# Attention weights and layer 0's head outputs turned in 32 by 32 blocks on VectorE and through DRAM, in a two-layer transformer trunk

## Chip, core and metric

The program runs on one core of a Trainium2 chip. A core has five engines that run their own instruction queues side by side: TensorE (PE, matmul), VectorE (DVE), ScalarE (ACT), GpSimd (POOL) and SyncE (SP, which here only starts DMAs). The metric is device time in microseconds (us). Lower is better.

## What is computed

Two transformer layers over 256 tokens of width 2048, all in float32. Layer 0 has differential attention (8 heads, each the difference of two softmax maps, then an RMS norm per head), layer 1 has forgetting attention (16 heads); each layer has a squared-ReLU MLP of width 8192. The parts that the change touches:

```python
a = p[:, :, 0] - lam * p[:, :, 1]                  # layer 0: weights of one head
o = jnp.einsum('bhqk,bhkv->bhqv', a, v)            # layer 0: sum over keys k
o = rmsnorm(o, subln_g, SUBLN_EPS) * (1.0 - lambda_init)
h = h + o.reshape(B, S, D_MODEL) @ w_o_a           # sum over the features of o
...
p = jax.nn.softmax(s, axis=-1)                     # layer 1
o = jnp.einsum('bhqk,bhkd->bhqd', p, v)            # layer 1: sum over keys k
h = h + o.reshape(B, S, D_MODEL) @ w_o_b
h = h + jnp.square(jax.nn.relu(rmsnorm(h) @ w_in)) @ w_out
```

TensorE sums over the partition of both operands. The softmax leaves the weights with queries on partitions, and the sum over keys needs keys there. So each head's weights have to be turned, and in layer 0 the outputs too (tokens on partitions, features wanted).

## The kernel before

All matrix products with the large weights run in split precision: a weight block `raw` is cast to `whi` (ACT, `split`, L173), `wlo = raw - whi` is formed (DVE, `split_low`, L176), and TensorE sums three products.

The program is one list of **slots**. A slot is one granule of weights: 512 KB, 128 by 1024. A unit of kind B (`mm_b`) has slots of 12 matmuls of 512 columns; a unit of kind A (`mm_a`) has four slots, with 8, 24, 8 and 24 matmuls. In the attention stages the units follow in the order V (8 slots), q, k, q, k (4 slots each) for two layer 0 heads, or V, k, q, k, q for two layer 1 pairs of heads; so heads follow each other by turns after 8 and 16 slots. Attention itself is cut into small steps that `plan(e)` hangs on later slots (e is the last slot of the head's last unit). Each slot s emits, in this order:

1. `pre[s]`: evacuations,
2. the cast of granule s+4 on ACT,
3. `mid[s]`: DVE steps of attention,
4. `split_low` of granule s+4 on DVE, and then on SP the load of granule s+8 into the `raw` buffer that this has just freed (`NRAW` = 4 buffers, L163),
5. the slot's matmuls,
6. `post[s]`: small PE steps.

Every engine works through its own instructions strictly in that order, so a step that waits holds everything behind it on its engine. The queue of SP holds the weight loads of the whole program.

For a layer 0 head: `scores` in `post[e+2]`, `softmax` in `mid[e+3]` and `mid[e+4]`, `weights` in `mid[e+4]` and `mid[e+5]`, `turn_a` (three TensorE transposes into PSUM) in `post[e+6]`, `keep_a` (an ACT copy to SBUF) in `pre[e+7]`, `av` (the product with V) in `post[e+7]`, `take_o` in `pre[e+8]`, `norm_o` in `mid[e+9]`, `turn_o` (four TensorE transposes) in `post[e+10]`, `split_o` in `pre[e+11]`. Layer 1 works on pairs of heads in the same manner, with six transposes in a `turn_a`; its `av` writes features on partitions, so its outputs need no turn. For the last two of the eight pairs `av` comes later (`e_av`), since V is made last there. At `pre[e+6]` of each second pair but the last, `spread_c` loads the next group's decay table (`NC`, 256 KB and 512 KB) on SP's queue.

Of the kernel before, what the change touches and what calls it, by code (L numbers as in the profile page):

```python
# [20 lines left out]
P = 128  # L21
D = 2048
S = 256
HD = 128
FF = 8192
NA = 8
# [16 lines left out]
def kernel(ctx: ExitStack, tc: tile.TileContext, *args):  # L43
    (x, rel_table, w_qkv, lq1, lk1, lq2, lk2, w_o_a,
     w_k, w_v, w_f, b_f, w_q, w_o_b, w_in, w_out, fin_g, onehot, xt, gcols, out) = args
    nc = tc.nc
# [18 lines left out]
    ident = sb.tile([P, P], F32, tag="ident", name="ident")  # L65
# [56 lines left out]
    g_sub = G[:, 80:82]  # L122
# [3 lines left out]
    pre, mid, post = (defaultdict(list) for _ in range(3))  # L126
# [102 lines left out]
    def split_turned(c, tps, gain, dst, bs=(0, 1)):  # L229
# [5 lines left out]
        for b, j, k in at:  # L235
            nc.vector.scalar_tensor_tensor(out=dst[2 * c + b][:, j, S:2 * S], in0=tps[b][:, j * S:(j + 1) * S],
                                           scalar=gain[:, k:k + 1], in1=dst[2 * c + b][:, j, 0:S],
                                           op0=ALU.mult, op1=ALU.subtract)

    def banks():  # L240
        return [ps.tile([P, 512], F32, tag="tp", name="tp") for _ in range(2)]

# [27 lines left out]
    class Norm:  # L270
# [96 lines left out]
    vt = {}  # L367
# [15 lines left out]
    def qk_done(key, R, tag, then=None):  # L383
# [5 lines left out]
                then(e)  # L389
        return done  # L390

    def diff_head(hd):
        p, hl = hd // 2, hd % 2
        st = {}
# [41 lines left out]
            return run  # L436

        def turn_a():
            t = ps.tile([P, 512], F32, tag="tp", name="tpa")
            nc.tensor.transpose(t[:, 0:P], st["a", 0][:, 0, 0:P], ident)  # L440
            nc.tensor.transpose(t[:, P:2 * P], st["a", 1][:, 0, 0:P], ident)
            nc.tensor.transpose(t[:, 2 * P:3 * P], st["a", 1][:, 0, P:2 * P], ident)
            st["tpa"] = t

        def keep_a():
            t = sb.tile([P, 3 * P], F32, tag="aT", bufs=4, name="aT")
            nc.scalar.copy(out=t, in_=st["tpa"][:, 0:3 * P])
            st["aT"] = t

        def av():  # L450
            o = ps.tile([P, 2, S], F32, tag="sc", name="o")
            a, v = st["aT"], vt["a", p]
            cs = slice(hl * S, (hl + 1) * S)
            nc.tensor.matmul(o[:, 0, :], a[:, 0:P], v[:, 0, cs], start=True, stop=True)
            nc.tensor.matmul(o[:, 1, :], a[:, P:2 * P], v[:, 0, cs], start=True, stop=False)
            nc.tensor.matmul(o[:, 1, :], a[:, 2 * P:3 * P], v[:, 1, cs], start=False, stop=True)
            st["o"] = o

        def take_o():
# [14 lines left out]
                                        scalar2=None, op0=ALU.mult)  # L474

        def turn_o():
            t = ps.tile([P, 512], F32, tag="tp", name="tpo")
            for v in range(2):
                for qt in range(2):
                    nc.tensor.transpose(t[:, (v * 2 + qt) * P:(v * 2 + qt + 1) * P],  # L480
                                        st["osb"][:, qt, v * P:(v + 1) * P], ident)
            st["tpo"] = t

        def split_o():
            d = new_x(f"hx{hd}")
            for v in range(2):
                src = st["tpo"][:, v * S:(v + 1) * S]
                nc.scalar.activation(out=d[:, v, 0:S], in_=src, func=AF.Copy, scale=g_sub[:, v:v + 1])
                nc.vector.scalar_tensor_tensor(out=d[:, v, S:2 * S], in0=src, scalar=g_sub[:, v:v + 1],
                                               in1=d[:, v, 0:S], op0=ALU.mult, op1=ALU.subtract)  # L490
# [245 lines left out]
    def fox_pair(g, i):  # L736
# [45 lines left out]
            return run  # L782

        def turn_a():
            for c in range(2):
                t = ps.tile([P, 512], F32, tag="tp", name="tpa")
                nc.tensor.transpose(t[:, 0:P], st["a", 0][:, c, 0:P], ident)
                nc.tensor.transpose(t[:, P:2 * P], st["a", 1][:, c, 0:P], ident)
                nc.tensor.transpose(t[:, 2 * P:3 * P], st["a", 1][:, c, P:2 * P], ident)
                st["tpa", c] = t  # L790

        def keep_a():
            for c in range(2):
                t = sb.tile([P, 3 * P], F32, tag="aT", bufs=4, name="aT")
                nc.scalar.copy(out=t, in_=st["tpa", c][:, 0:3 * P])
                st["aT", c] = t

        def av():
            o = ps.tile([P, 2, S], F32, tag="sc", name="o")
            v = vt["f", g]  # L800
            for c in range(2):
                a = st["aT", c]
                cs = slice((2 * i + c) * P, (2 * i + c + 1) * P)
                nc.tensor.matmul(o[:, c, :], v[:, 0, cs], a[:, 0:S], start=True, stop=False)  # L804
                nc.tensor.matmul(o[:, c, P:S], v[:, 1, cs], a[:, S:S + P], start=False, stop=True)  # L805
            st["o"] = o

        def split_o():
# [288 lines left out]
```

## Time and profile before

| What | Value |
|---|---|
| Median of 3 runs | 2205.89 us (2205.86 to 2207.84) |
| The profiled execution, its own time | 2205.36 us |
| Its span, first to last instruction | 2203.7 us |
| PE busy | 2191.5 us, 99% |
| DVE busy | 1362.5 us, 62% |
| ACT busy | 1015.7 us, 46% |
| DMA queue of SP (share of 16 engines) | 59.4%, 413.66 MB |
| Granted TensorE clock | 0.999 of full speed |

The span is 1.7 us shorter than the execution's own time, and that is 0.5 us below the median. PE busy counts the modelled length of matmuls that overlap, so what one matmul costs is read from the distance between two starts, not from its length.

### The profile page before, as it was taken

How to read it: one execution, taken by the hardware profiler on the slowest of the kernel's cores; microseconds unless marked ns; L12 is line 12 of the kernel's file. 1: busy time of each engine (PE TensorE's matmuls, PEld its weight loads, DVE VectorE, ACT ScalarE, POOL GpSimd, SP SyncE). 2: the span in 40 equal slices, each digit the busy share in tenths (PEclk: the TensorE clock that was granted, in tenths of full speed). 3: DMA queues.
4: the chain of work that ended last, by engine and by line, in shares of the span. 5: the costliest groups of instructions: out<-in, count | busy, mean ns of one | idle time of the engine just before them, and what ended most of it. 6: DMA issues, size and time to landing. Idle time of an engine off the chain costs nothing.

```text
span 2203.7 us, 28919 instructions
## 1 busy us (share of the span) xinstructions
PE 2191.5 (99%) x11242; PEld 1875.4 (85%) x11242; DVE 1362.5 (62%) x1769; ACT 1015.7 (46%) x1331; POOL 13.9 (1%) x19
## 2 busy tenths in 40 slices
PE   9999999999999999999999999999999999999998
PEld 7888888888888888888888888888888888888886
DVE  7666665665565565566576656657656645655655
ACT  6554555443444344345554444454434434443443
POOL 0000000000000000000001000000000000000000
PEclk9999999999999999999999999999999999999999
DMA  8655556556656656665656565555665566566664
GB/s 278 208 174 174 178 163 191 183 189 198 187 190 199 186 189 199 189 189 183 196 175 190 171 201 182 182 172 194 202 196 178 188 208 180 188 206 183 189 202 134
DMA packets 319224, 416.60 MB, mean 189 GB/s; under 512 B 15288, under 2 KB 217584, under 8 KB 318960
## 3 DMA queue, kind: packets, MB, share of 16 engines
q1 hardware_dynamic: 317888, 413.66, 59.4%
q8 instruction: 88, 1.44, 0.3%
q10 hardware_dynamic: 1200, 1.10, 0.2%
q14 instruction: 48, 0.39, 0.1%
HBM read 412.58 MB, written 2.13 MB: 188 GB/s over the span
## 4 chain that ended last, share of the span: by engine, by line
PE 98%; DMA 1%; DVE 0%; ACT 0%; SPq 0%; issue 0%; DVEq 0%; ACTq 0%
PE acc L203 32%; PE acc L207 17%; PE acc L187 15%; PE acc L189 15%; PE acc L188 15%; DMA raw<-in_w_qkv_a 1%; PE sc L402 0%; PE sc L746 0%; PE tp L226 0%; PE sc L188 0%; PE sc L187 0%; PE sc L189 0%; PE o L804 0%; DMA tab<-in_rel_bias_table 0%; PE fp L617 0%; PE o L805 0%
## 5 line engine op out<-in xcount | busy, mean ns | idle before, releaser
L176 DVE TENSOR_TENSOR wlo<-raw,whi 128x1024 fp32r<-128x1024 f32 x767 | 927.1, 1226 | 694.6 <-ACT whi L173 648.8
L173 ACT CAST whi<-raw 128x1024 fp32r<-128x1024 f32 x767 | 791.6, 1049 | 790.1 <-PE acc L189 441.3
L203 PE MATMUL acc<-x,whi 128*128 128x512 f32 x2816 | 659.0, 390 | 0.0
L203 PEld LDWEIGHTS acc<-x,whi 128*128 128x128 f32 x2816 | 522.8, 188 | 104.8
L187 PE MATMUL acc<-whi,hx 128*128 128x512 f32 x1120 | 436.8, 390 | 0.0
L189 PE MATMUL acc<-whi,hx 128*128 128x512 f32 x1120 | 435.8, 389 | 0.0
L188 PE MATMUL acc<-wlo,hx 128*128 128x512 f32 x1120 | 435.7, 389 | 0.0
L207 PE MATMUL acc<-x,wlo 128*128 128x256 f32 x2816 | 358.0, 284 | 0.0
L207 PEld LDWEIGHTS acc<-x,wlo 128*128 128x128 f32 x2816 | 351.6, 191 | 7.5
L189 PEld LDWEIGHTS acc<-whi,hx 128*128 128x128 f32 x1120 | 210.2, 188 | 43.9
L188 PEld LDWEIGHTS acc<-wlo,hx 128*128 128x128 f32 x1120 | 210.3, 188 | 43.4
L187 PEld LDWEIGHTS acc<-whi,hx 128*128 128x128 f32 x1120 | 210.2, 188 | 43.3
L588 ACT CAST hx<-s 128x512 fp32r<-128x512 f32 x64 | 39.8, 622 | 143.3 <-DVE s L586 143.3
L187 PE MATMUL acc<-whi,x 128*128 128x512 f32 x256 | 103.1, 403 | 0.7 <-ACT whi L953 0.7
L188 PE MATMUL acc<-wlo,x 128*128 128x512 f32 x256 | 100.6, 393 | 0.0
L189 PE MATMUL acc<-whi,x 128*128 128x512 f32 x256 | 100.6, 393 | 0.0
L312 ACT COPY z<-acc 128x512 f32<-128x512 f32 x96 | 56.3, 587 | 63.6 <-PE acc L203 63.5
L313 DVE TENSOR_TENSOR zs<-acc,z 128x512 f32<-128x512 f32 x96 | 66.4, 692 | 9.9 <-ACT z L312 1.9
L589 DVE TENSOR_TENSOR hx<-s,hx 128x512 fp32r<-128x512 f32 x64 | 44.3, 693 | 44.0 <-ACT hx L588 44.0
L324 DVE TENSOR_TENSOR h<-acc,h 128x512 f32<-128x512 f32 x88 | 56.7, 686 | 14.9 <-PE acc L189 14.9
L203 PE MATMUL acc<-hx,whi 128*128 128x512 f32 x256 | 61.1, 390 | 0.0
L187 PEld LDWEIGHTS acc<-whi,x 128*128 128x128 f32 x256 | 48.6, 190 | 12.8 <-ACT whi L953 2.3
(176 smaller groups left out, 1133.7 us busy)
## 6 DMA issues: line engine op xcount, KB each, us to landing
raw<-in_w_mlp_in SPq DMA_DIRECT2D x256, 512.0 KB, 3.8
raw<-in_w_mlp_out SPq DMA_DIRECT2D x256, 512.0 KB, 4.2
raw<-in_w_qkv_a SPq DMA_DIRECT2D x95, 512.0 KB, 4.4
raw<-in_w_o_a SPq DMA_DIRECT2D x32, 512.0 KB, 4.3
raw<-in_w_v_b SPq DMA_DIRECT2D x32, 512.0 KB, 3.7
raw<-in_w_k_b SPq DMA_DIRECT2D x32, 512.0 KB, 3.8
raw<-in_w_q_b SPq DMA_DIRECT2D x32, 512.0 KB, 3.7
raw<-in_w_o_b SPq DMA_DIRECT2D x32, 512.0 KB, 3.6
```

Source lines behind the costliest of these rows:

```text
L173: nc.scalar.copy(out=g.hi, in_=g.raw)
L176: nc.vector.tensor_tensor(out=g.lo, in0=g.raw, in1=g.hi, op=ALU.subtract)
L187: nc.tensor.matmul(bank[m], xh, hi[:, j, :], start=k == 0, stop=False)
L188: nc.tensor.matmul(bank[m], xh, lo[:, j, :], start=False, stop=False)
L189: nc.tensor.matmul(bank[m], xl, hi[:, j, :], start=False, stop=k == nk - 1)
L203: nc.tensor.matmul(bank[n], u.gs[i].hi[:, w], xt, start=k == 0, stop=k == 15)
L207: nc.tensor.matmul(bank[n][:, 0:S], u.gs[i].lo[:, w], xt[:, 0:S], start=False, stop=False)
L312: nc.scalar.copy(out=z1, in_=u.acc[:, :, S:2 * S])
L313: nc.vector.tensor_tensor(out=zs, in0=u.acc[:, :, 0:S], in1=z1, op=ALU.add)
L324: nc.vector.tensor_tensor(out=h[c][:, m, :], in0=u.bank[m], in1=h[c][:, m, :], op=ALU.add)
L588: nc.scalar.copy(out=t[:, :, 0:S], in_=s)
L589: nc.vector.tensor_tensor(out=t[:, :, S:2 * S], in0=s, in1=t[:, :, 0:S], op=ALU.subtract)
```

## The change

- `turn_a` leaves TensorE. It becomes DVE instructions that transpose 32 by 32 blocks (`to_blocks`), emitted in `mid[e+5]` right behind the weights. Each block is then turned, but stands in the wrong place.
- A trip through DRAM puts the blocks in their places: `send_a` in `pre[e+6]` writes them to a DRAM tile (one DMA in layer 0, two in layer 1), and four DMAs, one for each group of 32 partitions, read them back in `pre[e+7]` (`back_a` in layer 0; in layer 1 `keep_a`, straight into `aT`). All are issued on SP.
- In layer 0 ACT copies the result into `aT` in `pre[e+9]`. `av` moves from `post[e+7]` to `post[e+9]` in both layers (the last two pairs keep their slots).
- Layer 0's `take_o` and `norm_o` follow two slots later. `turn_o` is replaced for the first seven heads: `blocks_o` (two DVE transposes) in `mid[e+11]`, `send_o` (one DMA) in `pre[e+12]`, the way back (four DMAs) in `pre[e+13]`, `split_o` in `pre[e+15]`. The eighth head keeps its four TensorE transposes.
- `split_o` reads SBUF instead of PSUM, and its DVE half has four instructions of 128 columns instead of two of 256. Layer 1's two ACT copies in a `keep_a` are gone.

The diff, cut to its core (`diff_head` first, then `fox_pair`):

```diff
+    def to_blocks(b, src):
+        nc.vector.transpose(out=b.rearrange("p b k j -> p k b j"), in_=src)
+
+    def blocks_out(tag, *bs):
+        X = dr.tile([P, 4, sum(b.shape[2] for b in bs) * 32], F32, tag=tag, bufs=2, name=tag)
+        at = 0
+        for b in bs:
+            n = b.shape[2] * 32
+            nc.sync.dma_start(out=X[:, :, at:at + n], in_=b.rearrange("p b k j -> p b (k j)"))
+            at += n
+        return X
+
+    def blocks_in(r, X):
+        for b in range(4):
+            nc.sync.dma_start(out=r[32 * b:32 * b + 32].rearrange("p a k j -> p a (k j)"),
+                              in_=X[:, b, :].rearrange("(a i) x -> i a x", i=32))
...
         def turn_a():
-            t = ps.tile([P, 512], F32, tag="tp", name="tpa")
-            nc.tensor.transpose(t[:, 0:P], st["a", 0][:, 0, 0:P], ident)
-            nc.tensor.transpose(t[:, P:2 * P], st["a", 1][:, 0, 0:P], ident)
-            nc.tensor.transpose(t[:, 2 * P:3 * P], st["a", 1][:, 0, P:2 * P], ident)
-            st["tpa"] = t
+            b = four(scratch()[:, 512:896], 3)
+            to_blocks(b[:, :, 0:1, :], tiled(st["a", 0][:, 0, 0:P]))
+            to_blocks(b[:, :, 1:3, :], tiled(st["a", 1][:, 0, :]))
+            st["aB"] = b
...
-            post[e + 6].append(turn_a)
-            pre[e + 7].append(keep_a)
-            post[e + 7].append(av)
-            pre[e + 8].append(take_o)
-            mid[e + 9].append(norm_o)
-            post[e + 10].append(turn_o)
-            pre[e + 11].append(split_o)
+            mid[e + 5].append(turn_a)
+            pre[e + 6].append(send_a)
+            pre[e + 7].append(back_a)
+            pre[e + 9].append(keep_a)
+            post[e + 9].append(av)
+            pre[e + 10].append(take_o)
+            mid[e + 11].append(norm_o)
+            if hd < NA - 1:
+                mid[e + 11].append(blocks_o)
+                pre[e + 12].append(send_o)
+                pre[e + 13].append(keep_o)
+                pre[e + 15].append(split_o)
+            else:
+                post[e + 12].append(turn_o)
+                pre[e + 13].append(split_o)
...
-            post[e + 6].append(turn_a)
+            mid[e + 5].append(turn_a)
+            pre[e + 6].append(send_a)
             pre[e + 7].append(keep_a)
             post[e_av].append(av)
...
-                plan(e, e + 7 if g < 3 else e + 17 - 7 * i)
+                plan(e, e + 9 if g < 3 else e + 17 - 7 * i)
```

How this moves instructions. On PE, in the four slots after head 0's weights (`tpa` is the PSUM tile of the transposes, `aT` the turned weights), the three transposes go and the product with V leaves its place:

```order
 L207 MATMUL acc<-x_129,wlo 128x256 x4
-L440 MATMUL tpa<-ident,e 128x128
-L441 MATMUL tpa<-ident,e 128x128
-L442 MATMUL tpa<-ident,e 128x128
 L207 MATMUL acc<-x_130,wlo 128x256 x4
 L207 MATMUL acc<-x_131,wlo 128x256 x4
-L454 MATMUL o<-v,aT 128x256
-L455 MATMUL o<-v,aT 128x256
-L456 MATMUL o<-v,aT 128x256
 L207 MATMUL acc<-x_132,wlo 128x256 x4
```

It comes back (L507 to L509) two slots further on, behind the first slot of the next V unit.

On SP, at the same head, one DMA out and four back in stand between the weight loads (`aX` is the DRAM tile; DMAHW0 to 7 are eight semaphores that DMAs take in turn and that tell of their landing):

```order
 L165 DMA raw<-in_w_qkv_a 128x2x512 [waits DMAHW4_49,DVE_49]
+L250 DMA aX<-room 128x384
 L165 DMA raw<-in_w_qkv_a 128x2x512 [waits DMAHW5_49,DVE_49]
-L85 DMA h_109<-in_x 128x2x512
-L165 DMA raw<-in_w_qkv_a 128x2x512 [waits DMAHW6_49,DVE_49]
+L256 DMA room<-aX 32x4x96 [waits DMAHW2_49]
+L256 DMA room<-aX 32x4x96
+L256 DMA room<-aX 32x4x96 [waits DMAHW6_49]
+L256 DMA room<-aX 32x4x96 [waits DMAHW7_49]
+L85 DMA h_109<-in_x 128x2x512 [waits DMAHW0_49]
+L165 DMA raw<-in_w_qkv_a 128x2x512 [waits DMAHW1_49,DVE_49]
```

The first of the four waits for the landing of the DMA out (DMAHW2), and the next weight load, which stood directly behind its forerunner, now stands behind all four.

On DVE, from the norm of head 0 to the weights of head 1, before:

```order
L473 TENSOR_SCALAR osb<-osb,orstd 128x256 x2
L176 TENSOR_TENSOR wlo<-raw,whi 128x1024 x2
L489 SCALAR_TENSOR_TENSOR hx_931<-tpo,gains,hx_931 128x256 x2
L412 SCALAR_TENSOR_TENSOR ssb<-sc,T 128x2x128
L415 TENSOR_REDUCE nm<-ssb 128x2
L176 TENSOR_TENSOR wlo<-raw,whi 128x1024
L412 SCALAR_TENSOR_TENSOR ssb<-sc,T 128x512
```

and with the change:

```order
L526 TENSOR_SCALAR osb<-osb,orstd 128x256 x2
L243 STREAM_TRANSPOSE room<-osb 128x2x4x32 x2
L458 SCALAR_TENSOR_TENSOR ssb<-sc,T 128x2x128
L461 TENSOR_REDUCE nm<-ssb 128x2
L176 TENSOR_TENSOR wlo<-raw,whi 128x1024
L458 SCALAR_TENSOR_TENSOR ssb<-sc,T 128x512
```

Head 0's norm, which stood two slots ahead of head 1's softmax with two `split_low` in between, now stands in the same slot right ahead of it, with the block transposes of the outputs between them.

## Rows read from the trace of the kernel before

**Rows 1.** The page: busy time of the engines; the chain that ended last.

```profile
PE 2191.5 (99%) x11242; PEld 1875.4 (85%) x11242; DVE 1362.5 (62%) x1769; ACT 1015.7 (46%) x1331; POOL 13.9 (1%) x19
...
PE 98%; DMA 1%; DVE 0%; ACT 0%; SPq 0%; issue 0%; DVEq 0%; ACTq 0%
```

**Rows 2.** Groups by line on PE: count, busy us, mean ns, idle before.

```profile
L789 PE MATMUL tpa<-ident,e 128*128 128x128 f32 x16 | 4.4, 272 | 0.0
```

**Rows 3.** Timeline of PE around head 1's transposes: start us, length us, instruction.

```profile
98.34 0.27 PE L440 MATMUL tpa<-ident,e 128*128 128x128 f32 x1
...
98.59 0.47 PE L187 MATMUL acc<-whi,x 128*128 128x512 f32 x1
98.90 0.39 PE L188 MATMUL acc<-wlo,x 128*128 128x512 f32 x1
```

**Rows 4.** Groups by line and shape on DVE: plain operations of 256 columns.

```profile
L433 DVE SCALAR_TENSOR_TENSOR e<-e,rr 128x256 f32<-128x256 f32 x8 | 3.9, 485 | 0.3
...
L431 DVE TENSOR_SCALAR e<-e,rr 128x256 f32<-128x256 f32 x8 | 2.8, 353 | 0.3
```

**Rows 5.** Timeline of ACT: the end of head 0's `take_o`, and the next cast.

```profile
77.30 0.19 ACT L465 ACTIVATION_READ_ACCUMULATOR junk<-osb 128x1 f32 x1
78.61 1.05 ACT L173 CAST whi<-raw 128x1024 fp32r<-128x1024 f32 x1 [1.12 <-PE acc L203]
```

**Rows 6.** Timeline of PE at five places: `av` of head 0, and starts of slots.

```profile
75.18 0.59 PE L456 MATMUL o<-v,aT 128*128 128x256 f32 x2
75.43 0.83 PE L207 MATMUL acc<-x,wlo 128*128 128x256 f32 x4
...
82.94 0.39 PE L187 MATMUL acc<-whi,x 128*128 128x512 f32 x1
...
105.47 2.43 PE L203 MATMUL acc<-x,whi 128*128 128x512 f32 x10
...
1179.95 0.39 PE L187 MATMUL acc<-whi,x 128*128 128x512 f32 x1
...
1202.39 3.79 PE L203 MATMUL acc<-x,whi 128*128 128x512 f32 x16
```

**Rows 7.** Timeline of DVE from head 0's norm to head 1's weights.

```profile
82.38 0.16 DVE L255 TENSOR_SCALAR rs_v<-oss 128x2 f32<-128x2 f32 x1
...
84.75 2.36 DVE L176 TENSOR_TENSOR wlo<-raw,whi 128x1024 fp32r<-128x1024 f32 x2
...
88.44 0.41 DVE L412 SCALAR_TENSOR_TENSOR ssb<-sc,T 128x256 f32<-128x256 f32 x1
...
94.97 1.22 DVE L176 TENSOR_TENSOR wlo<-raw,whi 128x1024 fp32r<-128x1024 f32 x1
```

**Rows 8.** Timeline of DVE behind the weights of head 0 and of layer 1's first two pairs.

```profile
70.99 2.57 DVE L176 TENSOR_TENSOR wlo<-raw,whi 128x1024 fp32r<-128x1024 f32 x2
...
1167.21 1.22 DVE L176 TENSOR_TENSOR wlo<-raw,whi 128x1024 fp32r<-128x1024 f32 x1
...
1190.80 1.23 DVE L176 TENSOR_TENSOR wlo<-raw,whi 128x1024 fp32r<-128x1024 f32 x1 [0.77 <-ACT whi L173]
```

**Rows 9.** DMA issues by tensor: count, KB each, median us from issue to landing.

```profile
raw<-in_w_o_b SPq DMA_DIRECT2D x32, 512.0 KB, 3.6
...
NC<-C SPq DMA_DIRECT2D x4, 512.0 KB, 6.4
out<-h SPq DMA_DIRECT2D x8, 256.0 KB, 2.5
...
C<-fg_nc SPq DMA_DIRECT2D x1, 16.0 KB, 4.8
```

**Rows 10.** Timeline of SP where the decay table makes a trip through DRAM.

```profile
1145.25 0.49 SPq L696 DMA_DIRECT2D C<-fg_nc  x1
...
1150.11 0.37 SPq L729 DMA_DIRECT2D NC<-C  x1
1150.53 0.50 SPq L730 DMA_DIRECT2D NC<-C  x1
```

More of the change, by code (lines that the diff above doesn't have):

```diff
@@ L238, in split_turned, with four, by_turn, high_part @@
                                            op0=ALU.mult, op1=ALU.subtract)
+    def to_blocks(b, src):
[12 more added lines that the diff above has]
+                              in_=X[:, b, :].rearrange("(a i) x -> i a x", i=32))
+    def four(t, k):
+        return t.rearrange("p (b k j) -> p b k j", b=4, k=k)
+    def by_turn(t):
+        return t.rearrange("p (m a j) -> p m a j", a=4, j=32)
+    def high_part(d, src, view, gain):
+        out = view(d[:, 0:S]) if view else d[:, 0:S]
+        nc.scalar.activation(out=out, in_=src, func=AF.Copy, scale=gain)
+    def low_part(d, src, view, gain):
+        hi, lo = d[:, 0:S], d[:, S:2 * S]
+        at = [(view(lo)[:, m], src[:, m], view(hi)[:, m]) for m in range(2)] if view else [(lo, src, hi)]
+        for out, x, y in at:
+            nc.vector.scalar_tensor_tensor(out=out, in0=x, scalar=gain, in1=y, op0=ALU.mult, op1=ALU.subtract)
     def banks():
@@ L438, in turn_a, with send_a, back_a @@
         def turn_a():
[L439 to L443 removed]
+            b = four(scratch()[:, 512:896], 3)
+            to_blocks(b[:, :, 0:1, :], tiled(st["a", 0][:, 0, 0:P]))
+            to_blocks(b[:, :, 1:3, :], tiled(st["a", 1][:, 0, :]))
+            st["aB"] = b
+        def send_a():
+            st["aX"] = blocks_out("aX", st["aB"])
+        def back_a():
+            st["aR"] = four(scratch()[:, 1536:1920], 3)
+            blocks_in(st["aR"], st["aX"])
         def keep_a():
[L446 to L447 removed]
+            t = sb.tile([P, 3, P], F32, tag="aT", bufs=2, name="aT")
+            nc.scalar.copy(out=t.rearrange("p k (a j) -> p k a j", a=4), in_=st["aR"].rearrange("p a k j -> p k a j"))
             st["aT"] = t
@@ L481, in turn_o, with blocks_o, send_o, keep_o @@
                                         st["osb"][:, qt, v * P:(v + 1) * P], ident)
-            st["tpo"] = t
+            st["oT"] = [(t[:, v * S:(v + 1) * S], None) for v in range(2)]
+        def blocks_o():
+            b = scratch()[:, 0:512].rearrange("p (b v q j) -> p b v q j", b=4, v=2, q=2)
+            for qt in range(2):
+                to_blocks(b[:, :, :, qt, :], tiled(st["osb"][:, qt, :]))
+            st["oB"] = four(scratch()[:, 0:512], 4)
+        def send_o():
+            st["oX"] = blocks_out("oX", st["oB"])
+        def keep_o():
+            t = four(scratch()[:, 1024:1536], 4)
+            blocks_in(t, st["oX"])
+            st["oT"] = [(t[:, :, 2 * v:2 * v + 2, :].rearrange("p a q j -> p q a j"), by_turn) for v in range(2)]
         def split_o():
@@ L486, in split_o @@
             for v in range(2):
[L487 to L490, printed above, removed]
+                high_part(d[:, v, :], *st["oT"][v], g_sub[:, v:v + 1])
+            for v in range(2):
+                low_part(d[:, v, :], *st["oT"][v], g_sub[:, v:v + 1])
             oT["a", hd] = d
@@ L784, in turn_a, with send_a @@
         def turn_a():
+            b0 = sb.tile([P, 4, 2, 32], F32, tag="osb", bufs=2, name="aB0")
+            to_blocks(b0, st["a", 0][:, :, 0:P].rearrange("p c (b j) -> p c b j", j=32))
+            b1 = sb.tile([P, 4, 4, 32], F32, tag="osb", bufs=2, name="aB1")
             for c in range(2):
[L786 to L790, printed above, removed]
+                to_blocks(b1[:, :, 2 * c:2 * c + 2, :], tiled(st["a", 1][:, c, :]))
+            st["aB"] = b0, b1
+        def send_a():
+            st["aX"] = blocks_out("aX", *st["aB"])
         def keep_a():
[L793 to L796, printed above, removed]
+            t = sb.tile([P, 4, 6, 32], F32, tag="aT", bufs=2, name="aT")
+            blocks_in(t, st["aX"])
+            st["aT"] = t
         def av():
             o = ps.tile([P, 2, S], F32, tag="sc", name="o")
-            v = vt["f", g]
+            v, a = vt["f", g], st["aT"]
             for c in range(2):
-                a = st["aT", c]
                 cs = slice((2 * i + c) * P, (2 * i + c + 1) * P)
-                nc.tensor.matmul(o[:, c, :], v[:, 0, cs], a[:, 0:S], start=True, stop=False)
-                nc.tensor.matmul(o[:, c, P:S], v[:, 1, cs], a[:, S:S + P], start=False, stop=True)
+                nc.tensor.matmul(by_turn(o[:, c, :]), v[:, 0, cs],
+                                 a[:, :, c:3 + 2 * c:2 + c, :].rearrange("p a q j -> p q a j"), start=True, stop=False)
+                nc.tensor.matmul(o[:, c, P:S].rearrange("p (a j) -> p a j", a=4), v[:, 1, cs],
+                                 a[:, :, 3 + 2 * c, :], start=False, stop=True)
             st["o"] = o
```

13 lines of the change are left out of this document (10 added, 3 removed).

## The prediction

> **What bounds the kernel now.** I read the page first: PE is busy for 99% of the span, and 98% of the chain that ended last lies on PE [rows 1]. There is no second engine in that chain worth naming, so whatever PE is spared comes off the time, and any wait that PE is given adds to it in full. Since busy times on PE are modelled lengths that overlap, I then took the cost of a transpose from starts in the timeline. After that I followed, in the timelines of DVE, ACT and PE, how long the new way of the weights takes and how much time the schedule leaves it. Everything else hangs on these two.
>
> **What PE is spared.** Eight heads with three transposes, seven with four and eight pairs with six make 24 + 28 + 48 = 100. From the first of three transposes to the second matmul behind them is 98.90 - 98.34 = 0.56 us; the matmul in between takes 0.227 (sixteen of them, 3.79 less the last one's own 0.39, over fifteen steps [rows 6]), so three cost 0.33 and one 0.11 [rows 3]. The step is the same in the other blocks, which stand beside matmuls of the same two kinds. 100 x 0.11 = 11.0 us, all of it on the path. The rows also give a length of 272 ns for each [rows 2]. The Trainium skill ("TensorE: Matmul & The Clock Gate", Part 4: PE-mode transpose) speaks of about 275 ns for one in a kernel's context; the length agrees, and by it the saving would be 27.5 us, but a start follows the one before it after 0.11, so I don't take it.
>
> The products with V are only moved, and their operands keep their sizes; layer 1's moving operand is now read in runs of 32 columns. No row shows a strided moving operand; I take no extra cost, since neither its columns nor its passes change, and keep a few tenths per pair in the range.
>
> **What is added, and what covers it.** DVE gets 8 x 2 + 7 x 2 = 30 block transposes in layer 0 and 8 x 3 = 24 in layer 1, and two more halves in each of seven `split_o`. No row shows a block transpose. Plain operations of 256 columns take 353 and 485 ns [rows 4]; I take 0.42 for 256 columns and 0.33 for 128, so 0.75 for a layer 0 `turn_a`, 0.85 for `blocks_o` and 1.26 for a layer 1 `turn_a`; between the ends of the rows this moves a `turn_a` by less than 0.3. In sum it is some 25 us on an engine that idles for 38% of the span [rows 1], so it matters only where it delays a chain. 123 small DMAs join SP's queue; one after another they start 0.42 apart [rows 10]. Behind the four that come back stand the weight loads, which are held until the DMA out has landed, some 3 us later than now. A load is issued four slots ahead of its cast (a slot is 12 x 0.227 = 2.7 on PE in kind B) and lands in 3.6 [rows 9], and the cast stands another four slots ahead of its matmuls, so this delay stays off PE.
>
> The cost is the chain itself: DVE transposes, write to DRAM, read back, ACT copy, `av`. `av` is queued on PE at a fixed place; if its operand is late, all matmuls behind it wait. For the two transfers the rows give these ends. A write that finds the queue free lands 2.5 after its issue (`out`, 256 KB), the one write that goes out behind a weight load lands after 4.8 (`C`, 16 KB) [rows 9]. Here the write always goes out right behind a load, which lands in 3.6, so I take it to land 0.15 behind that load, 3.75 after the load's issue. The reads find the queue free or nearly so: at most 4.8 again, at least 2.0 (a load's 3.6 less the 1.6 that 512 KB add at best); I take 2.3, nearest to the free write.
>
> *Even heads of layer 0* (0, 2, 4, 6). DVE has the weights at 70.99 [rows 8]. Transposes 0.75, `wlo` 1.22: 72.95; there SP issues the load, then the write. Landing 76.7; the last of four reads starts 3 x 0.42 later, 78.0; landing 80.3; ACT copy, about as long as half of a cast of 1.05 [rows 5], 80.8. PE comes to `av` at 82.94 less three transposes (0.33) and less `av` itself, which now lies ahead of this slot start: six passes of 0.215 (two in 0.59 with 0.38 for the last's end), 1.29 [rows 6]. That is 81.3: 0.5 to spare, no stall.
>
> *Odd heads of layer 0* (1, 3, 5, 7). Here the step of the even head before gets in the way. `av` of head 0 now ends at 82.94 - 0.33 = 82.6 on PE. ACT's `take_o` ends 2.06 later (77.49 against 75.43 [rows 5, 6]): 84.7. The cast behind it and `wlo`: 86.95. The norm, 84.75 - 82.38 = 2.37 [rows 7]: 89.3. `blocks_o`: 90.15. From the first softmax of head 1 to the end of its weights DVE works without a pause, 94.97 - 88.44 = 6.53 [rows 7]: 96.7, against 94.97 before. `turn_a` and `wlo`: 98.65. Then as above: write landed 102.4, last read started 103.7, landed 106.0, copied 106.5. PE would come to `av` at 105.47 + 8 x 0.227 = 107.29 [rows 6], less ten transposes (1.1) and `av` (1.29): 104.9. So PE waits 1.6 us. Three heads make 4.8; the last one has W_o's slots of kind B ahead of it, about 0.9 longer, and waits 0.7. Sum 5.5.
>
> *Layer 1.* First pair of a group: weights done at 1167.21 [rows 8], three transposes 1.26, `wlo` 1.22: 1169.7. Two writes in pieces of 256 and 512 bytes, for which I add 0.6: landed 1173.9. Last read started 1175.2, twice the bytes, 2.6: 1177.8. PE: 1179.95 [rows 6] - 0.66 - 1.3 = 1178.0. Just covered. Second pair: `wlo` at 1190.80 had waited 0.77 for ACT, so it slips by 0.5 only [rows 8] and ends at 1192.5; but here the decay table's 768 KB stand in the queue between write and reads. Its second DMA goes out at about 1194.1 and lands 6.4 later [rows 9], 1200.5; one more load and the reads behind it, 1.9: 1202.4. PE: 1202.39 + 1.82 - 0.66 - 1.3 = 1202.25 [rows 6]. About 0.2 late; the third of these is later by nearly 1 in its DVE work, so I take 0.5 each, 1.5. The last two pairs have a cover several slots long: nothing.
>
> **Sum.** -11.0 + 5.5 + 1.5 = -4.0 us. The profiled execution took 2205.36, so 2201.4; the median of the runs is 0.5 above it: **2201.9**. About 0.2% (4.4 us) is what a measurement can tell from no change, so this lies on the border of a gain that can be told.
>
> **The rivals.** All hang on one length, the way from DVE's last transpose to the landed reads, compared with what I took (x us longer or shorter).
>
> - *The trip is covered everywhere.* If write and reads together take 1.6 less (a write at 2.5 after its own issue, which is 0.85 less, and reads at 2.0 with quicker DVE transposes and issues), no `av` waits: -11.0, **2194.9**. For it speaks that every cover misses by less than 2 us; against it that the odd heads' DVE chain alone costs 1.7 of their cover, which no transfer gives back.
> - *The trip outlasts its cover: slower.* Place: the wait for `aT` in front of `av`. At x = 0 seven places are late or level, from 0.2 the three first pairs join, from 0.5 the even heads, so 14 places pay. The stalls reach the 11.0 saved at x of about 0.45, and the kernel is slower by over 0.2% from about 0.8. With a write like `C` (4.8 after its issue, which is 1.45 more than mine) x = 1.4, the stalls are 7.0 + 0.2 x 7 + 0.3 x 10 + 0.9 x 14 = 24, and the time is 2205.9 + 13 = **2219**. For it speaks `C`, the only write of this kind in the trace, whose read back was issued 4.86 after it [rows 10]; against it that a good deal of 512 KB loads stood before `C` at that place. The Trainium skill ("VectorE: DVE Perf Modes", Rules for kernel authors) says to keep a 128 by 128 transpose on TensorE where PSUM will do as destination, as it does here. That rule sides with this rival; no row decides it, as none shows the DVE way.
> - *Late weight loads.* SP is held some 3 us per trip, 23 times. If that reached PE even at the odd heads alone, by 1 us each beside the stalls above, the time would be 2206. Against it speaks the double cover of eight slots.
>
> **Chances.** Forecast, with x between about -0.5 and 0.6 (2197 to 2208): 0.50, of it 0.23 faster and 0.25 within 0.2%, 0.02 slower. Trip covered: 0.22, faster. Trip outlasts: 0.25, of it 0.05 still within 0.2% and 0.20 slower. Late loads: 0.03, within. So faster 0.45, same 0.33, slower 0.22. The range leaves out the deepest tails on both sides: 2195.5 to 2216.
>
> **What would show it.** On PE, no `tpa` rows and 4 transposes `tpo` left; the step between the matmuls around them back at 0.227 and 0.12. Idle time of PE ahead of `av`, put down to ACT `aT` in layer 0 and to DMA `aT` in layer 1: by my steps about 1.6 at heads 1, 3, 5, less at 7, none at even heads, tenths in layer 1. DVE's block transposes at 0.3 to 0.5. The write's landing 3.3 and the reads' 2.3 after issue. I would be wrong if even heads wait (trip too long), if odd heads don't (DVE chain or reads quicker), or if casts wait for `raw` (late loads).

## The result and the profile after

The kernel after takes **2243.6 us** (median of 4 runs, 2242.9 to 2244.9) against 2206.3 before (median of 4 runs as well): ratio 1.0172, interval 1.0160 to 1.0184. It is 37.4 us slower. The forecast was 2201.9, with 2216 as the upper end of its range.

The page of after: busy time of the engines, and the shares of the chain that ended last ([rows 1] show both of before).

```profile
PE 2195.2 (98%) x11142; PEld 1872.6 (84%) x11142; DVE 1376.4 (61%) x1837; ACT 1007.6 (45%) x1315; POOL 13.2 (1%) x19
...
PE 88%; DMA 6%; DVE 4%; SPq 1%; issue 1%; ACT 1%; DVEq 0%; ACTq 0%
```

TensorE has the 100 matmul instructions less that were promised, and VectorE is no busier in share. But the chain, which lay on PE for 98%, now leaves PE for 12% of the span, to DMAs, VectorE and SP's queue. The waits of after on PE say where (engine, line, output, what ended the wait; us in total, times, longest):

```profile
PE o L881 <- DMA aT<-aX: 20.1, 5, 6.7
PE o L507 <- ACT aT L500: 9.4, 5, 3.1
PE acc L187 <- ACT hx L268: 4.7, 1, 4.7
```

L507 is layer 0's `av`, L881 layer 1's, L187 the first W_o matmul that reads head 6's output. These 34.2 us are new. A second part doesn't show as a wait. Behind six of the waits the granted clock was at its lower level, for 3.41 us four times and 6.83 us twice. Four stretches of PE around one wait in after (window, length, busy us and count by engine, granted clock, DMA share, GB/s):

```profile
1182.11:1190.11 8.00, 8.00 (x51) 7.20 (x50) 4.80 (x6) 2.66 (x4) 0.00 (x0) 1.00 0.62 179
1217.40:1224.20 6.80, 2.17 (x10) 1.49 (x9) 1.70 (x2) 2.20 (x3) 2.56 (x2) 1.00 1.12 237
1224.84:1228.25 3.41, 3.41 (x12) 2.84 (x11) 0.69 (x1) 1.53 (x2) 0.00 (x0) 0.50 0.50 160
1228.25:1236.25 8.00, 8.00 (x51) 7.27 (x51) 2.61 (x3) 2.10 (x2) 0.00 (x0) 1.00 0.39 121
```

In the second PE idles for most of the time, in the third it has work again and does it at half the clock (1.2 instead of 2.4 GHz), in the fourth it is back at the higher level. Half of 3.41 is 1.7 us per short stretch, and the two long ones, in which PE had work for 4.7 and 5.1 us, cost half of that: 4 x 1.7 + 2.4 + 2.6 = 11.8 us by estimate. Before has no such stretch ahead of its last 8 us.

A third account agrees. I compared each step from start to start on PE with the median of the same pair of matmuls in the trace of before. By this estimate the steps of after lost some 47 us more than those of before. Less the 11 us that were saved this makes 36 of the 37.4 measured. Where this account is quoted by place below, it is called the excess.

DMA issues of after (count, KB each, median us from issue to landing):

```profile
aT<-aX SPq DMA_DIRECT2D x32, 96.0 KB, 3.0
...
NC<-C SPq DMA_DIRECT2D x4, 512.0 KB, 8.1
aX<-aB SPq DMA_DIRECT2D x8, 256.0 KB, 4.1
...
oX<-room SPq DMA_DIRECT2D x7, 256.0 KB, 4.4
room<-oX SPq DMA_DIRECT2D x28, 64.0 KB, 3.3
aX<-room SPq DMA_DIRECT2D x8, 192.0 KB, 4.3
room<-aX SPq DMA_DIRECT2D x32, 48.0 KB, 2.0
...
aX<-aB SPq DMA_DIRECT2D x8, 128.0 KB, 4.0
```

`aX` and `oX` are the DRAM tiles. The writes to them land after 4.0 to 4.4 us (medians), where 3.35 after their own issue was reckoned (0.15 behind a load, whose landing is in [rows 9]). Layer 0's reads take 2.0 for the weights and 3.3 for the outputs. The larger part of the decay table now takes 8.1, against 6.4 in [rows 9].

### The profile page after: what moved, and what is told of

Same layout as the page of the kernel before. It is cut to its first block, busy times and chain, and to the rows that moved or that the text cites. A ratio compares the mean times of both kernels' runs of the same rounds, so it can differ in the third digit from the quotient of the medians.

```text
span 2241.8 us, 28970 instructions
## 1 busy us (share of the span) xinstructions
PE 2195.2 (98%) x11142; PEld 1872.6 (84%) x11142; DVE 1376.4 (61%) x1837; ACT 1007.6 (45%) x1315; POOL 13.2 (1%) x19
## 4 chain that ended last, share of the span: by engine, by line
PE 88%; DMA 6%; DVE 4%; SPq 1%; issue 1%; ACT 1%; DVEq 0%; ACTq 0%
PE acc L203 30%; PE acc L207 15%; PE acc L187 13%; PE acc L189 13%; PE acc L188 13%; DVE wlo L176 2%; DMA aX<-aB 1%; DMA aT<-aX 1%; DMA aX<-room 1%; DMA raw<-in_w_qkv_a 1%; SPq L256 1%; DMA room<-aX 1%; PE o L881 1%; PE tp L226 0%; PE sc L821 0%
## 5 line engine op out<-in xcount | busy, mean ns | idle before, releaser
L187 PE MATMUL acc<-whi,hx 128*128 128x512 f32 x1120 | 437.7, 391 | 4.7 <-ACT hx L268 4.7
L187 PEld LDWEIGHTS acc<-whi,hx 128*128 128x128 f32 x1120 | 210.7, 188 | 48.6 <-ACT hx L268 5.1
L187 PE MATMUL acc<-whi,x 128*128 128x512 f32 x256 | 103.5, 404 | 0.6 <-ACT whi L1033 0.6
L187 PEld LDWEIGHTS acc<-whi,x 128*128 128x128 f32 x256 | 48.9, 191 | 12.9 <-ACT whi L1033 2.1
```

Of the source, the lines that this page charges most:

```text
L187: nc.tensor.matmul(bank[m], xh, hi[:, j, :], start=k == 0, stop=False)
```

## The experiments

Two theories stood against each other. COVER: the loss is a list of separate waits at the places where the trip is longer than its slots. LOAD: the trip's work slows the kernel as such. Times are medians; ratios are against the kernel before on the same chip. Beside these runs before took 2205.7 to 2206.0, beside after 2206.3, so what a run has less than after is good to some tenths of a us at best.

| run | us | ratio to before, interval |
|---|---|---|
| trip_unused | 2205.5 | 0.9998, 0.9989 to 1.0008 |
| no_turn | 2194.0 | 0.9945, 0.9931 to 0.9960 |
| l0_only | 2220.5 | 1.0072, 1.0056 to 1.0089 |
| l1_only | 2228.3 | 1.0103, 1.0088 to 1.0118 |
| table_behind | 2222.5 | 1.0077, 1.0063 to 1.0091 |
| table_act | 2225.4 | 1.0088, 1.0075 to 1.0102 |
| norm_later | 2232.7 | 1.0122, 1.0108 to 1.0136 |
| head6_pe | 2239.7 | 1.0163, 1.0145 to 1.0182 |
| three_fixes | 2205.8 | 1.0005, 0.9996 to 1.0015 |
| cover | 2199.8 | 0.9975, 0.9965 to 0.9985 |
| cover2 | 2195.0 | 0.9950, 0.9938 to 0.9963 |

### The trip's load alone, and what TensorE is spared

`trip_unused`, on the kernel before (the helpers of after added; `blocks_a`, `send_a`, `blocks_o` and `send_o` do what `turn_a`, `send_a`, `blocks_o` and `send_o` do in after, `back_a` and `back_o` read the result into SBUF; `turn_a` is TensorE's, as before; the outputs' trip stands two slots earlier than in after, since the norm does; for room in SBUF the two `osb` buffers are one tile):

```diff
+            mid[e + 5].append(blocks_a)
+            pre[e + 6].append(send_a)
+            pre[e + 7].append(back_a)
             post[e + 6].append(turn_a)
...
+                mid[e + 9].append(blocks_o)
+                pre[e + 10].append(send_o)
+                pre[e + 11].append(back_o)
```

> The kernel before with its TensorE transposes, and beside them the whole trip of after (block transposes on VectorE, write to DRAM, reads back, in the same slots of the plan), whose result nobody reads. It prices the trip's load alone, with no wait for it. COVER: nothing, 2206, within 2204 and 2210, and no wait for weights. LOAD: most of the 48 us lost by after is here too: 2235 to 2255, with TensorE waiting for weights (raw, whi, wlo) or for softmax results that come later.

Measured 2205.5, the time of before. The page's chain is that of before:

```profile
PE 98%; DMA 1%; DVE 0%; ACT 0%; issue 0%; DVEq 0%; SPq 0%; ACTq 0%
```

And among the DMA issues between 1200 and 1220 us, where a decay table passes, a read of the trip lands as late as in after:

```profile
osb<-aX SPq DMA_DIRECT2D x1, 96.0 KB, 7.7
```

So 54 block transposes, 123 DMAs and 12,800 KB cost nothing that can be measured as long as nobody waits for them. LOAD falls here, and with it the third rival of the prediction, late weights: ScalarE's casts wait longer for `raw` in this run (31.5 us in sum, 13.2 before), but TensorE doesn't.

`no_turn`, on the kernel before (the same edit in layer 1 and for `tpo`):

```diff
-            nc.tensor.transpose(t[:, 0:P], st["a", 0][:, 0, 0:P], ident)
-            nc.tensor.transpose(t[:, P:2 * P], st["a", 1][:, 0, 0:P], ident)
-            nc.tensor.transpose(t[:, 2 * P:3 * P], st["a", 1][:, 0, P:2 * P], ident)
+            st["tpa"] = st["a", 0][:, 0, 0:P], st["a", 1][:, 0, 0:2 * P]
```

> The kernel before, with the 100 transposes left out on TensorE and nothing in their place: ScalarE and VectorE copy the unturned tiles from SBUF, so the weights and layer 0's outputs stay unturned (that part of the computation is changed). It prices what TensorE is spared if nothing is waited for. By the start-to-start times of [rows 3], 100 x 0.11 = 11.0 us: 2195.3, between 2193.5 and 2197. If the blocks cost more than their start-to-start times show (275 ns each, as the Trainium skill's page TensorE: Matmul & The Clock Gate states in Part 4 for a transpose): 2178.8.

Measured 2194.0, 12.0 us less than before. The expectation miscounted: this kernel leaves out head 7's four as well, so 104 transposes, and one is worth 0.115 us. That is the start-to-start price of [rows 3], not the length of 272 ns in [rows 2], nor the figure of about 275 ns that the Trainium skill ("TensorE: Matmul & The Clock Gate", Part 4) gives for a transpose in a kernel's context; by it the run would have come out at 2177 by estimate.

### One layer at a time

`l0_only` has layer 1 as before, `l1_only` layer 0.

> Layer 0 as in the kernel after, layer 1 as before. Two theories. COVER: the trip (block transposes, write, reads) is longer than the slots that the plan leaves it, TensorE waits for its result, and the clock is halved for some us behind the longer waits. LOAD: the trip's own work (3,000 KB more on SP's queue, 20 us more on VectorE, elements kept by ScalarE) delays the rest of the kernel wherever it stands. COVER: by the excess that the trace of after shows place by place, layer 0 loses 12.8 us at the products by V and 6.5 us at the first W_o group that reads head 6's output, and spares 52 x 0.11 = 5.7 us of TensorE: 2206.3 + 19.3 - 5.7 = 2219.9, between 2217 and 2223. LOAD: the loss follows the bytes moved; layer 0 moves 8 x 2 x 192 + 7 x 2 x 256 = 6,656 KB of 12,800, about half of the 48.4 us that were lost in all, so 2206.3 + 25.2 - 5.7 = 2225.8, with waits for weights and not only for the turned tiles.

> Layer 0 as before, layer 1 as in the kernel after. COVER: layer 1 loses 4.2 + 6.0 + 0.5 + 8.2 + 0.3 + 8.8 = 28.0 us by the places of the trace of after, and spares 48 x 0.11 = 5.3 us: 2206.3 + 28.0 - 5.3 = 2229.0, between 2226 and 2232; the changes that this run and the one of layer 0 alone show against before add up to the 37.4 us of the whole change within 2 us. LOAD: about half of 48.4 us less 5.3 us: 2224, and the two parts add up to less than the whole, since the load then is spread thinner.

Measured +14.6 and +22.4 us, together 37.0 of 37.4. COVER had said +13.6 and +22.7. The waits keep to their places. Waits on PE in `l0_only`:

```profile
PE o L507 <- ACT aT L500: 9.5, 5, 3.1
PE acc L187 <- ACT hx L268: 3.2, 1, 3.2
```

And in `l1_only`, where L852 is layer 1's `av`:

```profile
PE o L852 <- DMA aT<-aX: 21.2, 6, 7.9
```

(The "3,000 KB" in the expectation of `l0_only` should read 12,800, as its own sum has it; the argument doesn't use it.)

### Layer 1's second pairs: what stands ahead of the reads

Timeline of SP in after around the second pair of the first group (start, length, instruction):

```profile
1209.41 0.37 SPq L165 DMA_DIRECT2D raw<-in_w_q_b  x1
1209.83 1.21 SPq L250 DMA_DIRECT2D aX<-aB  x2
1211.08 0.74 SPq L804 DMA_DIRECT2D NC<-C  x1
1211.87 0.63 SPq L805 DMA_DIRECT2D NC<-C  x1
1212.59 0.66 SPq L165 DMA_DIRECT2D raw<-in_w_q_b  x1
1214.70 2.42 SPq L256 DMA_DIRECT2D aT<-aX  x4
```

PE at this pair's `av`, with its wait in brackets:

```profile
1224.21 0.67 PE L881 MATMUL o<-aT,v 128*128 128x256 f32 x2 [4.65 <-DMA aT<-aX]
```

And the DMA issues from 1208 to 1226 us, with their medians to landing:

```profile
raw<-in_w_q_b SPq DMA_DIRECT2D x4, 512.0 KB, 8.6
...
aT<-aX SPq DMA_DIRECT2D x4, 96.0 KB, 7.9
...
aX<-aB SPq DMA_DIRECT2D x1, 128.0 KB, 4.0
```

The four reads go out from 1214.70 on, as soon as the write has landed, and yet they take 7.9 us: 768 KB of table and a 512 KB load went into the queue ahead of them. The three second pairs are not alike, though. In the second group the write, which is ahead of the table in the queue, is itself late. DMA issues of after from 1290 to 1299 us:

```profile
aX<-aB SPq DMA_DIRECT2D x1, 256.0 KB, 7.7
```

The reads behind it take 5.4 us there. Two small edits ask what holds the reads. `table_behind` issues the table one slot later:

```diff
-                    pre[e + 6].append(lambda: spread_c(g + 1))
+                    pre[e + 7].append(lambda: spread_c(g + 1))
```

> The kernel after, with the next group's decay table issued one slot later, behind the four reads of the second pair's trip. QUEUE: in the second pairs the reads stand on SP's queue behind a 768 KB table and land 7.5 to 8.5 us after their issue, where they take 2.1 to 3.0 us in the first pairs; so the three second pairs, which lose 6.0 + 8.2 + 8.8 = 23.0 us, fall to what first pairs lose (0.3 to 4.2 us each): about 5 us in all, 2243.6 - 18 = 2225.6, between 2221 and 2231. LOADS: it is the weight loads ahead of the reads that hold them, and the table only adds to it; then the reads still land late, and no more than a third of the 23 us comes back: 2236 to 2243.

Measured 2222.5, 21.1 us less than after. DMA issues of `table_behind` from 1208 to 1221 us: the reads of the same pair land in 3.1 us.

```profile
aT<-aX SPq DMA_DIRECT2D x4, 96.0 KB, 3.1
```

Its waits on PE: of 20.1 us for layer 1's `aT` 4.9 are left.

```profile
PE o L881 <- DMA aT<-aX: 4.9, 5, 1.7
```

LOADS falls: the weight loads stand ahead of the reads as in after. `table_act` keeps the place in the program and changes the engine that issues the table, and with it the queue:

```diff
-        nc.sync.dma_start(out=t[:, :, 0:P], in_=C[:, 0:P].unsqueeze(0).broadcast_to([P, 4, P]))
-        nc.sync.dma_start(out=t[:, :, P:3 * P], in_=C.unsqueeze(0).broadcast_to([P, 4, S]))
+        nc.scalar.dma_start(out=t[:, :, 0:P], in_=C[:, 0:P].unsqueeze(0).broadcast_to([P, 4, P]))
+        nc.scalar.dma_start(out=t[:, :, P:3 * P], in_=C.unsqueeze(0).broadcast_to([P, 4, S]))
```

> The kernel after, with the decay tables issued at the same place of the plan, but by ScalarE, on a queue of its own; the reads of the trip stay on SP's queue. QUEUE: the reads land late since they stand behind the table in one queue in order; on two queues they land in 2 to 3 us as in the first pairs, and the time is that of table_behind, 2222.5, between 2220 and 2227. ENGINES: the reads land late since the table's 768 KB fill the 16 DMA engines, whichever queue brought them; then the reads still take 5 us and more, and at most a third of the 21 us comes back: 2236 to 2244.

Measured 2225.4, inside QUEUE's range. But the run doesn't separate QUEUE from ENGINES, since it moves the table in time as well. ScalarE comes to this point of the program earlier than SP does. The table's second DMA on ScalarE's timeline of this run (ACTq is ScalarE issuing a DMA):

```profile
1206.38 0.52 ACTq L805 DMA_DIRECT2D NC<-C  x1
```

SP at the reads:

```profile
1215.58 2.48 SPq L256 DMA_DIRECT2D aT<-aX  x4
```

How long the table's two DMAs took to land here:

```profile
DMA to landing us min/median/max: 4.6/5.5/6.4
```

And the DMA issues from 1207 to 1221 us:

```profile
aT<-aX SPq DMA_DIRECT2D x4, 96.0 KB, 2.5
...
aX<-aB SPq DMA_DIRECT2D x1, 128.0 KB, 5.8
```

The table has landed by 1212.8, 2.8 us before the reads go out; in the other two groups it has too. In after it went out 2.8 us before them. So both edits show the same thing: the reads are quick where the table isn't being moved in front of them. Whether in after the order of one queue held them or the share of the DMA engines that the table took stays open; the number that QUEUE forecast came out without a test of QUEUE. The Trainium skill ("DMA: Bandwidth & Descriptors", Queues, rings and completion order) says that each DMA engine takes packets in turn from the queues that have work; no run here shows it for the reads. What does overlap with the table on the other queue is the write, which takes 5.8 here and 4.0 in after. Layer 1's `aT` is waited for 8.2 us in this run, 3.3 more than in `table_behind`, about the 2.8 us between the two medians, whose intervals against before overlap.

### Layer 0's odd heads: what stands ahead on VectorE

Timeline of VectorE in after, from head 0's norm to head 1's block transposes:

```profile
88.93 0.61 DVE L526 TENSOR_SCALAR osb<-osb,orstd 128x256 f32<-128x256 f32 x2
89.45 0.76 DVE L243 STREAM_TRANSPOSE room<-osb 128x256 f32<-128x256 f32 x2
90.14 0.38 DVE L458 SCALAR_TENSOR_TENSOR ssb<-sc,T 128x256 f32<-128x256 f32 x1
...
96.64 0.63 DVE L243 STREAM_TRANSPOSE room<-e 128x128 f32<-128x128 f32 x2
97.19 2.32 DVE L176 TENSOR_TENSOR wlo<-raw,whi 128x1024 fp32r<-128x1024 f32 x2
```

SP behind it, with the write of head 1's weights at 99.81 and their reads from 104.07:

```profile
96.94 1.75 SPq L256 DMA_DIRECT2D room<-oX  x4
98.79 0.98 SPq L165 DMA_DIRECT2D raw<-in_w_qkv_a  x1
99.81 0.51 SPq L250 DMA_DIRECT2D aX<-room  x1
...
104.07 2.02 SPq L256 DMA_DIRECT2D room<-aX  x4
```

And PE at head 1's `av`:

```profile
108.28 0.86 PE L507 MATMUL o<-v,aT 128*128 128x256 f32 x2 [2.77 <-ACT aT L500]
```

The order is the one that the prediction followed: head 0's norm and `blocks_o` end at 90.2 and only then does head 1's softmax begin; the block transposes are done at 97.3. `norm_later` turns it round for heads 0, 2 and 4:

```diff
-            mid[e + 11].append(norm_o)
+            late = 3 if hd in (0, 2, 4) else 0
+            mid[e + 11 + late].append(norm_o)
```

(and `blocks_o`, `send_o`, `keep_o` and `split_o` by `late` as well).

> The kernel after, with norm_o, blocks_o and the output's trip of heads 0, 2 and 4 three slots later, so that they stand on VectorE behind the odd head's turn_a and not in front of its softmax. ORDER: the odd heads 1, 3 and 5 lose 4.5 + 2.8 + 3.2 = 10.5 us, since their block transposes come late from VectorE; behind the edit they lose what the even heads lose, 0.6 to 1.0 us each: 2243.6 - 8 = 2235.6, between 2233.5 and 2238. LANDING: the wait is the write's landing, 4.2 to 4.5 us where 3.35 was reckoned, whatever VectorE's order; then nothing changes, 2243.6.

Measured 2232.7, 10.9 us less than after; ORDER had said 8, with 2233.5 as the lower end of its range. Of its waits on PE, that for layer 0's `aT`, 9.4 us in after, is now

```profile
PE o L507 <- ACT aT L500: 1.5, 3, 0.6
```

and the slow stretch behind head 1's wait is gone too. By the excess the odd heads gave back 8.8 us and the even ones 1.0; the rest is less than the 2 us by which layer 1's excess differs between these two profiles. LANDING falls: the write still takes 4.3 us (median).

### W_o's first unit and head 6

Timeline of ScalarE in after at head 6's high part:

```profile
329.43 0.91 ACT L268 ACTIVATE hx<-room,gains 128x256 fp32r<-128x256 f32 x2 [5.78 <-DMA room<-oX]
```

And of PE behind it:

```profile
329.99 0.50 PE L187 MATMUL acc<-whi,hx 128*128 128x512 f32 x1 [4.71 <-ACT hx L268]
```

`head6_pe` leaves that head's output on TensorE:

```diff
-            if hd < NA - 1:
+            if hd < NA - 2:
```

> The kernel after, with head 6's output turned on TensorE like head 7's. The first W_o unit reads this output in the slot in which the trip's result is only split, and waits 4.9 us there, with a stretch at half clock behind: 6.5 us in all. COVER: they come back, less 4 transposes of 0.12 us: 2243.6 - 6.5 + 0.5 = 2237.6, between 2236 and 2239. If W_o's wait has another cause (a late weight, head 7 behind it), it stays: 2243 to 2245.

Measured 2239.7, 3.9 us less than after, above the expected 2236 to 2239. Its runs lie between 2236.8 and 2247.6, so the time by itself doesn't tell it from after. The trace does: between 300 and 345 us no matmul waits any more, and this place's excess falls from 6.8 to 0.3 us. Part of what it gave back is lost elsewhere in this profile: behind the waits of heads 1 and 3, which stay, the lower clock lasts 6.83 and 3.41 us, where after has 3.41 and none.

### All three, and a version with room

`three_fixes` has the edits of `table_behind`, `norm_later` and `head6_pe`, and moves no `av`.

> The kernel after with the edits of table_behind, norm_later and head6_pe together; the users of the trips keep their slots. ADD: the three are separate waits, so their gains add up: 21.1 + 10.9 + 3.9 to 6.0 of 2243.6 leaves 2205.6 to 2207.7, between 2202 and 2209, about the time before: the sparing of TensorE just pays for the small waits that are left. If the waits hide one another, less than 30 us come back: over 2213.

Measured 2205.8, ratio 1.0005: the time of before. Its runs lie between 2202.9 and 2214.4. The three gains add up, 37.8 us together against 21.1 + 10.9 + 3.9 = 35.9 one by one. In the profile, which is of the shortest run, 5.2 us of waits for the trip are left on PE (3.4 and 1.8), the longest 0.9, and no slow stretch behind any.

`cover` goes the other way about. The weights' trip keeps its slots and the table its harmful place; the users are moved. In layer 0 the norm and the outputs' trip follow the product with V, so they too come later, for heads 0, 2 and 4 by the three slots of `norm_later`:

```diff
-            pre[e + 9].append(keep_a)
-            post[e + 9].append(av)
-            pre[e + 10].append(take_o)
-            mid[e + 11].append(norm_o)
+            n = 12 if hd < NA - 1 else 10
+            pre[e + n].append(keep_a)
+            post[e + n].append(av)
+            pre[e + n + 1].append(take_o)
+            mid[e + n + 2].append(norm_o)
...
-        order.extend((u, i, (0, 1)) for u in us[:2] for i in range(n - 1))
-        order.extend((u, n - 1, (0, 1)) for u in us[:2])
+        last = 2 if kind == "a" else 1
+        order.extend((u, i, (0, 1)) for u in us[:2] for i in range(n - last))
+        order.extend((u, i, (0, 1)) for i in range(n - last, n) for u in us[:2])
...
-                plan(e, e + 9 if g < 3 else e + 17 - 7 * i)
+                plan(e, e + 12 if g < 3 else e + 17 - 7 * i)
```

> The kernel after with the same trip everywhere, and only its users later: the products by V 3 slots later in layer 0 (heads 0 to 6; head 7 one slot) and 3 slots later in the pairs of layer 1's first three groups, the normalisation behind them, and the granules of W_o that read the outputs of heads 6 and 7 behind all others of the first two units. The decay table keeps its place. COVER: no wait for a trip is left, and TensorE is spared what the kernel without transposes showed, 12.0 us of 2206.0, less head 7's four transposes (0.5 us): 2194.5, between 2192.5 and 2198. If the later users only pass the waits on (to PSUM banks that the scores need, to VectorE's later norm, to W_o): 2200 or more, with waits at scores or at W_o.

Measured 2199.8, faster than both kernels, but 5 us above the expectation and outside its range. One wait is left, and I had made it. Head 6's `split_o` now stood in front of head 7's `keep_a` on ScalarE, as its timeline shows:

```profile
325.53 0.91 ACT L268 ACTIVATE hx<-room,gains 128x256 fp32r<-128x256 f32 x2 [5.72 <-DMA room<-oX]
326.35 0.50 ACT L500 COPY aT<-room 128x384 f32<-128x384 f32 x1
```

PE comes to head 7's `av` only behind that copy:

```profile
326.90 0.70 PE L507 MATMUL o<-v,aT 128*128 128x256 f32 x2 [2.73 <-ACT aT L500]
```

`cover2` puts that one `split_o` two slots later:

```diff
-                pre[e + n + 6].append(split_o)
+                pre[e + n + (6 if hd < NA - 2 else 8)].append(split_o)
```

> The kernel of the run cover, with head 6's split_o two slots later still. In cover one wait for a trip is left: ScalarE stands 5.72 us at head 6's high part for room<-oX, head 7's keep_a stands behind it, and TensorE waits 2.7 us (4.8 us of excess with the slower stretch behind). COVER: that goes, and the time is cover's less 4 us: 2195.8, between 2194 and 2198; then TensorE has no wait for a trip at all, and what is left against the kernel without transposes (2194.0) is head 7's four transposes, 0.5 us, and small change. If the later split only holds TensorE at W_o: 2199 or more.

Measured **2195.0**, ratio 0.9950 (0.9938 to 0.9963), the fastest version of this case that still turns everything, 10.7 us below before with 100 transposes spared. A read of layer 1's trip takes up to 9.8 us in its profile, and no matmul waits for one. On its page the chain is back on PE:

```profile
PE 98%; DMA 1%; DVE 0%; ACT 0%; SPq 0%; issue 0%; DVEq 0%; ACTq 0%
```

## Why the prediction was wrong, step by step

The method was right: TensorE is the bound, one transpose spared is worth its step from start to start, and every late operand is paid in full. `cover2` has the time that the prediction gave for its first rival, a trip covered everywhere (2194.9), but not by that rival's way: there the trip was to be shorter, here its readers come later. The forecast failed on the size of the waits, on a reader that it left out and on the clock.

| step of the prediction | reckoned | measured |
|---|---|---|
| 100 transposes off PE | -11.0 us | 0.115 each in no_turn, -10.7 in cover2 |
| DVE: `turn_a`, `blocks_o` in layer 0 | 0.75, 0.85 | 0.63, 0.76 |
| write, issue to landing | 3.35 | 4.0 to 4.4 |
| reads in layer 0, of the weights | 2.3 | 2.0 |
| wait at an even head | 0 | 0 to 0.5 |
| wait at heads 1, 3, 5; 7 | 1.6 each; 0.7 | 2.8, 2.7, 3.1; none |
| W_o at head 6's output | not looked at | 4.7 |
| wait in a first pair | 0 | 2.1, 0.4, 0 |
| wait in a second pair | 0.5 each | 4.6, 6.3, 6.7 |
| clock behind a wait | not looked at | some 11.8 in all, by estimate |
| weights late | no | no |

**The odd heads: right mechanism, 1.2 us too small.** The prediction had SP's load go out when `wlo` has ended, at 98.65; it went out at 98.79. From there two things were longer. The load's issue took 0.98 where 0.42 was taken, so the write went out at 99.81 and not at 99.07; and the write took 4.2 us to land, not 3.35. That makes 1.6 us, and the reads gave none of it back: each landed after 2.2 to 2.3 us as reckoned, but the four issues lay further apart. `av` began at 108.28 instead of 106.5, 1.8 later; PE had come to it at 105.5 instead of 104.9, 0.6 later, so its wait grew by 1.2. For the last head 0.7 was reckoned; in after it doesn't wait, with the stall at W_o ahead of it, and without that stall, in `three_fixes`, it waits 0.3.

**The second pairs: the right place, the wrong length.** The prediction saw the table between write and reads and gave it 6.4 us from the issue of its second DMA, and 1.9 for the load and the reads behind it: 8.3 in all. In after that DMA went out at 1211.87 and `av` began at 1224.2, 12.3 later. The median of the table's larger part is 8.1 in after, and that of the loads in this stretch 8.6. The 6.4 of [rows 9] is the table's landing without the trip; in `table_behind`, where the reads go out ahead of it, it is 6.2 again. On ScalarE's queue in `table_act`, beside the trip's write, it is 7.6, so SP's queue alone doesn't make it long. The landing times of the trace of before didn't hold beside the transfers that the change adds. This term was 1.5 us and came to 17.6 of waits plus the slow stretches behind them. It is the largest error, and `table_behind` returns 21.1 us by one slot. (In the first pairs the prediction's own steps give a landing at 1174.05, not 1173.9, which leaves almost nothing of the cover; they waited 2.1, 0.4 and 0 us.)

**W_o: a step left out.** I followed the weights to `av` everywhere, but head 6's output not to its reader. W_o's first unit reads it in the very slot in which it is split. That cost 4.7 us of wait and, by estimate, 1.7 of clock.

**The clock: a step left out.** Each stall was priced at its own length. Six of them brought a stretch at half clock, which by the estimate above adds a third to the 34.2 us of waits. This part differs from run to run: heads 3 and 5 wait 2.7 and 3.1 us in after with no such stretch behind them, and 2.6 and 3.3 us in `table_behind` with one of 3.41 us each.

**The slower rival had the place but not the price.** It put the wait in front of `av` and let it decide from 0.8 us of a longer trip. From the last block transpose to the landed reads the way was some 1.8 us longer than reckoned at head 1 (97.3 to 107.7) and 0.8 at head 0 (71.7 to 81.1), so it is not one length, as the rivals had it. Even with 1.8 everywhere that rival's own scale makes 7.0 + 0.2 x 7 + 0.3 x 10 + 1.3 x 14 = 30 us of stalls and a time of about 2225. What lies beyond, to 2243.6, is the table in the second pairs, W_o and the clock. The stated range ended at 2216, below the 2219 that the prediction gave this rival. The Trainium skill's rule that I put beside it ("VectorE: DVE Perf Modes", Rules for kernel authors: a 128 by 128 transpose on TensorE where PSUM will do) agrees with after, but not with `cover2`, where the way over VectorE is 10.7 us faster; the measurement decides, and here the question was room in the plan, not the engine.

What stays open: whether the queue's order or the DMA engines' share held the reads behind the table; why a write lands in 4.0 to 4.4 us where the free one of [rows 9] took 2.5; and why waits of nearly the same length are followed by a slow stretch at one place or in one run and not in another. No run separates these.

## What to carry to other kernels

When a step leaves the bounding engine for a longer way round, price the way by where its transfers stand in their queue, and follow every result to its last reader; then move the readers before you touch the transfers. A trip whose load is free when nobody waits (`trip_unused`) is worth nearly all that is spared (10.7 of 11.5 us) as soon as each reader has the slots (`cover2`). And a small read that others wait for goes ahead of a large transfer that nobody needs soon (`table_behind`), or the large one goes out so early that it has landed by then (`table_act`).

## What the hardware showed that I had not expected

- A 96 KB read took 7.9 us behind 768 KB of table and a 512 KB load on one queue, 3.1 with the table behind it, and 2.5 where the table had landed 2.8 us before the read went out.
- A stall on TensorE costs more than its length: in after the granted clock was 0.50 for 3.41 or 6.83 us behind six waits of 2.1 to 6.7 us, although PE had work. Two waits of 2.7 and 3.1 us had no such stretch behind them.
- A write to DRAM of 128 to 256 KB landed after 4.0 to 4.4 us (medians; one took 7.7), so write and read back make 6.3 us at the weights of layer 0 (4.3 + 2.0), before the four issues.
